# Gate and up of a SwiGLU FFN with seven block products in place of eight, in a two-layer hybrid network on one core

## The chip, the cores and the metric

The kernel runs on one core of a Trainium2 chip: TensorE (PE, with its weight loads as PEld), VectorE (DVE), ScalarE (ACT), GpSimd (POOL) and SyncE (SP), the last two here only to issue DMAs and for a few small fills. The metric is the device time of one launch in microseconds. Three runs of the kernel before gave 1988.75, 1989.3 and 1994.19 us.

## The reference

Two layers, 512 tokens, 1024 features, all in fp32. Each layer is

```
x = x + 0.5 * ffn(rms_norm(x), w_gate, w_up, w_down)      # "f1"
x = x + mixer(rms_norm(x))                                # "mx"
x = x + 0.5 * ffn(rms_norm(x), ...)                       # "f2"
ffn(x) = (silu(x @ w_gate) * (x @ w_up)) @ w_down         # 1024 -> 2816 -> 1024
rms_norm(x) = x * rsqrt(mean(x*x) + 1e-6) * w
```

The mixer concatenates an mLSTM, a state-space branch and a differential attention, and ends in a product with w_out. Its arithmetic is not changed.

## The kernel before

x stays in SBUF, transposed, as eight tiles x0 to x7 of 128 features by 512 tokens. Phases run in the order f1, mx, f2, f1, mx, f2.

Products are made in three parts: an fp32 operand is split into a high part that ScalarE casts to fp32r (L121 for weights, L134 for x) and the remainder that VectorE subtracts (L122, L135); `mm3` (L126 to L129) then issues three matmuls into one PSUM bank: high by high, high by low, low by high. The weights are the stationary operand, x the moving one, 512 tokens wide. In the mixer's token projections x is stationary and 256 or 272 columns of weights move.

The hidden layer has 22 blocks f of 128 features. For each f, gate and up take 2 x 8 products of a 128x128 weight block with a feature tile, 48 matmuls; then L212 to L220 make the hidden block: both sums are scaled by the inverse root `rsb`, silu, product, split into gh and gl. The down products, 8 x 22 x 3 = 528 matmuls, follow when all 22 blocks are there. An FFN is 1584 matmuls of 128x512.

When an output tile x[d] is complete, `prep` (L131 to L141) makes the next phase's xh[d] and xl[d] at once and adds x[d] squared to `sqacc`. The norm's factor is not applied to x but to the sums, so a phase's products can begin before it exists. For the first block of an FFN the order is written for this: gate and up run interleaved over the feature tiles, and the matmul that sums `sqacc` over the features (L176) stands before the eighth tile's products. VectorE's Newton steps for the inverse root (L151 to L156, eleven operations) then run beside TensorE.

Each engine executes its instructions in the order in which the framework's scheduler put them; instructions made under `tc.high_priority()` (weight loads, splits) are moved ahead. Weights come by 1 MB loads on SyncE's queue into two `raw` buffers; GpSimd's queue carries the DMAs that accumulate into SBUF. The mixer has four `big` buffers (NBIG) for its tables, sums and the decay tiles D of its four heads: `decay(h)` loads a mask into D, accumulates a row onto it by a GpSimd DMA (L759) and exponentiates it, `scores(h)` multiplies into it, `value(h)` (L784) uses it.

Of the kernel before, what the change touches and what calls it, by code (L numbers as in the profile page):

```python
# [30 lines left out]
NBIG = 4  # L31
# [13 lines left out]
def hybrid_kernel(ctx, tc, aps, phases):  # L45
# [4 lines left out]
    res = ctx.enter_context(tc.tile_pool(name="res", bufs=1))  # L50
    wp = ctx.enter_context(tc.tile_pool(name="wp", bufs=1))
# [29 lines left out]
    raw0 = None  # L81
    with tc.high_priority():

        nc.sync.dma_start(out=pv, in_=aps["pv"])
        if phases[0][0] != "mx":
            raw0 = wp.tile([P, 2048], F32, name="raw", tag="raw", bufs=2)
        for d in range(KD):
            if raw0 is not None and d in (0, 1, 3, 4):
                c = slice((0, 1024, 0, 512, 1536)[d], (512, 1536, 0, 1024, 2048)[d])
                nc.sync.dma_start(out=raw0[:, c], in_=aps["wgu"][phases[0][1], int(phases[0][0] == "f2"), 0][:, c])  # L90
            nc.sync.dma_start(out=x[d], in_=aps["xT"][:, d, :])
        nc.sync.dma_start(out=cn, in_=aps["cn"])
        nc.sync.dma_start(out=bc, in_=aps["bc"])
# [10 lines left out]
    def load(src, soon=True):  # L104
        n = src.shape[1]
        with tc.high_priority() if soon else nullcontext():
            raw = wp.tile([P, 2 * WPC], F32, name="raw", tag="raw", bufs=2)
            nc.sync.dma_start(out=raw[:, :n], in_=src)
        return raw

    def split(raw, lo, n, eng=dve):
        return split_parts(raw, ((lo, n),), eng)

    def split_parts(raw, parts, eng=dve):
        with tc.high_priority():
            hi = wp.tile([P, WPC], F32R, name="whi", tag="whi", bufs=3)
            lw = wp.tile([P, WPC], F32R, name="wlo", tag="wlo", bufs=3)
            to = 0
            for lo, n in parts:
                t = slice(to, to + n)  # L120
                act.copy(hi[:, t], raw[:, lo:lo + n])  # L121
                eng.tensor_tensor(lw[:, t], raw[:, lo:lo + n], hi[:, t].bitcast(F32), ALU.subtract)  # L122
                to += n
        return hi, lw

    def mm3(out, lh, ll, rh, rl, first, last):  # L126
        pe.matmul(out, lh, rh, start=first, stop=False)  # L127
        pe.matmul(out, lh, rl, start=False, stop=False)  # L128
        pe.matmul(out, ll, rh, start=False, stop=last)  # L129


    def prep(d, wcol):
        w = pv[:, wcol + d:wcol + d + 1]
        act.activation(xh[d], x[d], AF.Copy, scale=w)  # L134
        dve.scalar_tensor_tensor(xl[d], x[d], w, xh[d].bitcast(F32), ALU.mult, ALU.subtract)  # L135
# [7 lines left out]
    def rstd(ssq, n, pool_=tp, src=None):  # L143
# [5 lines left out]
        v = pool_.tile(shape, F32, name="rs_v", tag="rs_v%d" % w)  # L149
        q = pool_.tile(shape, F32, name="rs_q", tag="rs_q%d" % w)  # L150
# [22 lines left out]
    def rms_everywhere(pool_):  # L173

        ps = aux()
        pe.matmul(ps, ones, sqacc, start=True, stop=True)  # L176
        rstd(rsb, DM, pool_, ps)


    def ffn(l, which, nxt, first):  # L180
        with tc.tile_pool(name=f"g{l}{which}", bufs=1) as gp:
            gh, gl = [], []
            for f in range(KF):
                if f == 0:
# [24 lines left out]
                if first and 5 <= f <= 11 and f % 2:
                    spread_bias(f // 2 - 2)  # L210
# [767 lines left out]
```

## Time and profile before

| | |
|---|---|
| three runs | 1988.75, 1989.3, 1994.19 us |
| profiled execution: its own time, its span | 1989.71 us, 1987.6 us |
| busy: TensorE, VectorE, ScalarE, GpSimd | 1971.1, 1013.4, 696.7, 49.6 us |
| first matmul | 8.44 us |
| f1, mixer, f2 of layer 0 | 364.70, 263.50, 360.90 us |
| f1, mixer, f2 of layer 1 | 361.30, 264.00, 364.80 us |
| DMA: bytes moved, mean rate | 209.12 MB, 105 GB/s |
| granted TensorE clock over the span | 1.000 |

The span runs from the first to the last instruction of the profiled execution. The six stages are cut where the first matmul of a phase starts; the last one contains the output's stores. A matmul's listed duration overlaps that of its neighbours, so its cost in a stream is the distance from one start to the next.

### The profile page before, as it was taken

What the parts mean: (1) busy time and instruction counts of PE and PEld (TensorE: products, weight loads), DVE (VectorE), ACT (ScalarE), POOL (GpSimd) and SP (SyncE); (2) the same over time, 40 slices, a digit from 0 to 9 for tenths busy, and PEclk for the clock granted to TensorE, in tenths of its full rate; (3) what the DMA queues carried; (4) which work ended last, traced back from release to release, by engine and by line L of the source; (5) the groups of instructions that cost most, each with busy time, mean ns of one, the idle gap of its engine ahead of it and who ended that gap; (6) DMA issues with size and microseconds to landing.
All of it is one profiled execution on the core that took longest, in us unless ns stands there. A gap on an engine that the chain in (4) does not pass through costs nothing.

```text
span 1987.6 us, 23535 instructions
## 1 busy us (share of the span) xinstructions
PE 1971.1 (99%) x9598; PEld 1646.2 (83%) x9598; DVE 1013.4 (51%) x1697; ACT 696.7 (35%) x1140; POOL 49.6 (2%) x95
## 2 busy tenths in 40 slices
PE   8999999999999999999999999999999999999999
PEld 6888888989888888888888888889898888888887
DVE  7444433478765644443354444334877665444322
ACT  4223322347644322322223222223476333322211
POOL 0000000020000000000000000000200000000000
PEclk9999999999999999999999999999999999999999
DMA  5323232456412222223222222224654132232331
GB/s 181 119 99 104 87 106 85 134 165 159 112 49 88 103 90 101 103 88 106 85 106 85 106 86 106 91 91 139 189 136 101 42 106 103 89 107 85 111 102 63
DMA packets 48071, 209.12 MB, mean 105 GB/s; under 512 B 4871, under 2 KB 17447, under 8 KB 27100
## 3 DMA queue, kind: packets, MB, share of 16 engines
q1 hardware_dynamic: 41148, 187.38, 27.5%
q0 software_dynamic: 6816, 20.25, 4.3%
q8 instruction: 75, 1.23, 0.3%
q14 instruction: 32, 0.26, 0.0%
HBM read 194.97 MB, written 7.66 MB: 102 GB/s over the span
## 4 chain that ended last, share of the span: by engine, by line
PE 97%; DMA 1%; ACT 1%; DVE 0%; issue 0%; SPq 0%; POOLq 0%
PE acc L129 18%; PE acc L127 18%; PE acc L128 17%; PE aux L127 13%; PE aux L129 13%; PE aux L128 13%; PE po L566 1%; PE aux L784 1%; DMA D<-cn 1%; PE po L772 1%; PE aux L534 0%; DMA D<-row_dram 0%; PE aux L655 0%; PE aux L555 0%; PE side L772 0%; PE aux L707 0%
## 5 line engine op out<-in xcount | busy, mean ns | idle before, releaser
L121 ACT CAST whi<-raw 128x1024 fp32r<-128x1024 f32 (+2 forms) x344 | 350.8, 1022 | 984.5 <-PE acc L128 424.5
L122 DVE TENSOR_TENSOR wlo<-raw,whi 128x1024 fp32r<-128x1024 f32 (+2 forms) x344 | 407.4, 1187 | 329.3 <-ACT whi L121 329.1
L127 PE MATMUL acc<-xh,whi 128*128 128x512 f32 x896 | 353.1, 394 | 8.4 <-ACT xh L134 8.4
L128 PE MATMUL acc<-xl,whi 128*128 128x512 f32 x896 | 351.0, 392 | 0.0
L129 PE MATMUL acc<-xh,wlo 128*128 128x512 f32 x896 | 350.2, 391 | 0.0
L127 PE MATMUL aux<-xh,whi 128*128 128x512 f32 x704 | 274.2, 390 | 0.0
L129 PE MATMUL aux<-xh,wlo 128*128 128x512 f32 x704 | 274.2, 389 | 0.0
L128 PE MATMUL aux<-xl,whi 128*128 128x512 f32 x704 | 274.1, 389 | 0.0
L127 PEld LDWEIGHTS acc<-xh,whi 128*128 128x128 f32 x896 | 168.5, 188 | 43.6 <-ACT xh L134 8.4
L128 PEld LDWEIGHTS acc<-xl,whi 128*128 128x128 f32 x896 | 168.6, 188 | 34.9 <-issue 1.0
L129 PEld LDWEIGHTS acc<-xh,wlo 128*128 128x128 f32 x896 | 168.6, 188 | 34.2
L215 DVE TENSOR_TENSOR us<-aux,rsb 128x512 f32<-128x512 f32 x88 | 60.8, 691 | 265.0 <-PE aux L129 264.9
L128 PEld LDWEIGHTS aux<-xl,whi 128*128 128x128 f32 x704 | 132.3, 188 | 27.8
L129 PEld LDWEIGHTS aux<-xh,wlo 128*128 128x128 f32 x704 | 132.3, 188 | 27.6
L127 PEld LDWEIGHTS aux<-xh,whi 128*128 128x128 f32 x704 | 132.4, 188 | 27.3
L212 DVE TENSOR_TENSOR gs<-acc,rsb 128x512 f32<-128x512 f32 x88 | 60.8, 691 | 170.9 <-PE acc L129 170.8
L127 PE MATMUL acc<-gh,whi 128*128 128x512 f32 x352 | 138.7, 394 | 0.0
L127 PE MATMUL aux<-gh,whi 128*128 128x512 f32 x352 | 138.7, 394 | 0.0
L129 PE MATMUL acc<-gh,wlo 128*128 128x512 f32 x352 | 138.0, 392 | 0.0
L129 PE MATMUL aux<-gh,wlo 128*128 128x512 f32 x352 | 138.0, 392 | 0.0
L128 PE MATMUL acc<-gl,whi 128*128 128x512 f32 x352 | 136.6, 388 | 0.0
L128 PE MATMUL aux<-gl,whi 128*128 128x512 f32 x352 | 136.6, 388 | 0.0
(273 smaller groups left out, 2552.9 us busy)
## 6 DMA issues: line engine op xcount, KB each, us to landing
raw<-wgu SPq DMA_DIRECT2D x87, 1024.0 KB, 4.8
raw<-wdn SPq DMA_DIRECT2D x44, 1024.0 KB, 4.8
raw<-win SPq DMA_DIRECT2D x12, 1024.0 KB, 6.5
raw<-winf SPq DMA_DIRECT2D x12, 1024.0 KB, 4.9
raw<-wout SPq DMA_DIRECT2D x8, 1024.0 KB, 5.0
st<-qk_dram POOLq DMA_DIRECT2D x24, 256.0 KB, 5.8
sS<-cn SPq DMA_DIRECT2D x8, 512.0 KB, 4.8
qk_dram<-hl POOLq DMA_DIRECT2D x16, 256.0 KB, 3.3
```

The costliest lines, as they stand in the source:

```text
L121: act.copy(hi[:, t], raw[:, lo:lo + n])
L122: eng.tensor_tensor(lw[:, t], raw[:, lo:lo + n], hi[:, t].bitcast(F32), ALU.subtract)
L127: pe.matmul(out, lh, rh, start=first, stop=False)
L128: pe.matmul(out, lh, rl, start=False, stop=False)
L129: pe.matmul(out, ll, rh, start=False, stop=last)
L212: dve.tensor_tensor(gs, pp[0], rsb, ALU.mult)
L215: dve.tensor_tensor(us, pp[1], rsb, ALU.mult)
L566: pe.matmul(po[:, h * 64:(h + 1) * 64], at["a", n][:, j * P:(j + 1) * P], dv[j][:, (2 * p + h) * 64:(2 * p + h + 1) * 64], start=j == 0, s ...
L772: pe.matmul(sp[:, :n], mk[h // 2][hp, j * P:(j + 1) * P], mq[h // 2][hp, j * P:S], start=True, stop=True)
L784: pe.matmul(pnv[:, n, :], D[:, at_(j, n)], V[:, j, h, :], start=j == 0, stop=j == n)
```

## The change

Gate and up are computed by a Strassen-Winograd scheme. Two blocks of hidden features and the feature tiles in pairs make a 2x2 matrix of weight blocks (11, 12, 21, 22), the two halves of the tokens and the tile pairs a 2x2 matrix of x. Instead of eight block products there are seven, between blocks or sums of blocks. The 22 hidden blocks become 11 pairs p, and each pair is seven steps in the order of `STEPS`; a step is one weight block, or sum of blocks, of 128x1024 for gate and up together, split into high and low part, and 24 matmuls of 256 columns (2 for gate and up, 4 tile pairs, 3 parts). The sums of weights are s1 = 21 + 22 and s4 = 12 + s2, made by a GpSimd DMA that accumulates onto a loaded block, and s2 = 11 - s1, s3 = 11 - 21, made by VectorE. In the very first FFN, pairs 0 and 1 have s1 and s4 from VectorE. X, Y and Z name PSUM banks in which the products accumulate; copies of three partial results (`sn`) are added to others, one of them by an accumulating DMA (into c3).

The sums of x are made once for a phase: `prep7` scales two feature tiles, makes the three plain blocks xR (high and low) and the four sums xT (high and low). For the first FFN `prep_all` does all eight tiles at once.

The down products no longer wait for all hidden blocks. Six blocks at a time (18 matmuls into the bank `side`) are put between the steps of the next three pairs, by the table `WHEN`; the last four blocks' (12 matmuls for a feature tile) stand at the end. Loads are of 512 KB or less, into four `raw` and six `rx` buffers. The mixer keeps three `big` buffers in place of four; weights are laid out in memory to suit. The factor 0.5 moves from the addition to x into the hidden block.

```diff
-NBIG = 4
+NBIG = 3
+CB, RX, HB = 2, 6, 5
+WHEN = ((3, 4, 6, 7, 9, 10, 12, 13), (3, 5, 7, 9, 11, 13, 15, 17))
...
+    def prep7(i, wcol, tmp, four):
+        if i == 0:
+            parts["xR"] = [handed(4 + n, [P, 4, 2, 256], F32R, f"xR{n}") for n in range(3)]
+            parts["xT"] = []
+        xT = handed(i, [P, 4, 2, 256], F32R, "xT")
+        parts["xT"].append(xT)
+        xw = four("xw")
+        for n in range(2):
+            w = pv[:, wcol + 2 * i + n:wcol + 2 * i + n + 1]
+            act.activation(xw[:, 2 * n:2 * n + 2].rearrange("p a b -> p (a b)"), x[2 * i + n], AF.Copy, scale=w)
+        for n, b in enumerate((0, 2, 3)):
+            r = parts["xR"][n][:, i]
+            act.copy(r[:, 0], xw[:, b])
+            dve.tensor_tensor(r[:, 1], xw[:, b], r[:, 0].bitcast(F32), ALU.subtract)
+        sums(four("xt"), xw, xT, dve)
+        for n in range(2):
+            square(2 * i + n, tmp)
+    def sums(t, b, out, eng):
+        eng.tensor_tensor(t[:, 0], b[:, 1], b[:, 0], ALU.subtract)
+        eng.tensor_tensor(t[:, 1], t[:, 0], b[:, 3], ALU.subtract)
+        eng.tensor_tensor(t[:, 2], b[:, 3], b[:, 1], ALU.subtract)
+        eng.tensor_tensor(t[:, 3], b[:, 2], t[:, 1], ALU.add)
+        act.copy(out[:, :, 0], t)
+        dve.tensor_tensor(out[:, :, 1], t, out[:, :, 0].bitcast(F32), ALU.subtract)
...
-    def rms_everywhere(pool_):
-        ps = aux()
-        pe.matmul(ps, ones, sqacc, start=True, stop=True)
-        rstd(rsb, DM, pool_, ps)
-    def ffn(l, which, nxt, first):
...
+    STEPS = (("11", 0, "X"), ("s1", 3, "Y"), ("s2", 4, "X"), ("s4", 2, "Y"), ("s3", 5, "X"), ("12", 1, "Z"), ("22", 6, "X"))
+    def ffn(l, which, nxt, first, ctx3):
+        wcol = l * PV_N + (PV_N2 if which else PV_N1)
+        fp = ctx3.enter_context(tc.tile_pool(name=f"f{l}{which}", bufs=1, reuse_waits="tile"))
...
+        def blocks_of(p):
+            w = aps["wgu"][l, which, p]
+            soon = not first or p > 1
+            r = {"11": loadx(w[0], soon)}
+            if soon:
+                r["s1"] = loadx(w[2])
+                with tc.high_priority():
+                    pool.dma_start(out=r["s1"], in_=w[3], accum_op=ALU.add)
+            return r
+        def rest_of(p, r):
+            w = aps["wgu"][l, which, p]
+            soon = not first or p > 1
+            r["21"] = loadx(w[2], soon)
+            if soon:
+                r["s4"] = loadx(w[1])
+            r["12"] = load(w[1], soon)
+            r["22"] = load(w[3], soon)
+        def prep_all():
...
+            prep_all()
+        xR, xT = parts["xR"], parts["xT"]
+        hF = {}
+        def x_of(f, k):
+            return xR[f][:, k] if f < 3 else xT[k][:, f - 3]
+        def rms():
+            ps = side()
+            pe.matmul(ps, ones, sqacc, start=True, stop=True)
+            rstd(rsb, DM, (tmp(), tmp()), ps)
+        def gate_up(p, after):
+            raws = raws0 if first and p == 0 else blocks_of(p)
+            rest_of(p, raws)
+            c = cbig("c")
+            ps, copies = {}, {}
+            for n, (name, f, where) in enumerate(STEPS):
+                if name not in raws and name != "s2" and name != "s3":
+                    a, b = ("21", "22") if name == "s1" else ("12", "s2")
+                    raws[name] = fp.tile([P, WPC], F32, name=name, tag="rx", bufs=RX)
+                    dve.tensor_tensor(raws[name], raws[a], raws[b], ALU.add)
+                if name in ("s2", "s3"):
+                    a, b = (raws["11"], raws["s1"]) if name == "s2" else (raws["11"], raws["21"])
+                    with tc.high_priority():
+                        raws[name] = fp.tile([P, WPC], F32, name=name, tag="S", bufs=2)
+                        dve.tensor_tensor(raws[name], a, b, ALU.subtract)
+                        if name == "s2" and "s4" in raws:
+                            pool.dma_start(out=raws["s4"], in_=raws["s2"], accum_op=ALU.add)
+                hi, lw = split(raws[name], 0, 1024)
+                if name in ("11", "s1", "s2"):
+                    copies[name] = fp.tile([P, 2, 256], F32, name="sn", tag="sn", bufs=4)
+                for s in range(2):
+                    new = (s, where) not in ps
+                    if new:
+                        ps[s, where] = (total() if s and p % 2 else acc()) if where == "X" else aux()
+                    out = ps[s, where][:, 0:256]
+                    for k in range(4):
+                        cc = slice(s * 512 + k * P, s * 512 + (k + 1) * P)
+                        r = x_of(f, k)
+                        mm3(out, hi[:, cc], lw[:, cc], r[:, 0], r[:, 1], new and k == 0, k == 3, True)
+                    if name in copies:
+                        act.copy(copies[name][:, s], out)
+                    elif name == "s4":
+                        dve.tensor_tensor(c[:, s, 1], out, copies["s2"][:, s], ALU.add)
+                    elif name == "s3":
+                        act.copy(c[:, s, 3], out)
+                    elif name == "12":
+                        dve.tensor_tensor(c[:, s, 0], out, copies["11"][:, s], ALU.add)
+                    else:
+                        act.copy(c[:, s, 2], out)
+                if name == "s3":
+                    pool.dma_start(out=c[:, :, 3], in_=copies["s1"], accum_op=ALU.add)
+                after(n)
+            rb = rsb.rearrange("p (a b) -> p a b", b=256)[:, None].broadcast_to([P, 2, 2, 256])
+            g, u = c[:, 0], c[:, 1]
+            for t in (g, u):
+                t4 = t.rearrange("p (m n) t -> p m n t", m=2)
+                dve.tensor_tensor(t4, t4, rb, ALU.mult)
+            act.activation(g, g, AF.Silu)
+            dve.scalar_tensor_tensor(u, g, 0.5, u, ALU.mult, ALU.mult)
+            hh = fp.tile([P, 4, 256], F32R, name="hh", tag="hh", bufs=HB)
+            hl = fp.tile([P, 4, 256], F32R, name="hl", tag="hl", bufs=HB)
+            act.copy(hh, u)
+            dve.tensor_tensor(hl, u, hh.bitcast(F32), ALU.subtract)
+            hF[p] = [(hh[:, 2 * n:2 * n + 2].rearrange("p a b -> p (a b)"),
+                      hl[:, 2 * n:2 * n + 2].rearrange("p a b -> p (a b)")) for n in range(2)]
+        def down(c, d, ps):
+            fs = range(6 * c, min(6 * c + 6, KF))
+            n = len(fs) * P
+            raw = load(aps["wd3"][l, which, c, d] if c < 3 else aps["wd2"][l, which, d])
+            hi, lw = split(raw, 0, n)
+            for i, f in enumerate(fs):
+                cc = slice(i * P, (i + 1) * P)
+                mm3(ps, hi[:, cc], lw[:, cc], *hF[f // 2][f % 2], i == 0, i == len(fs) - 1)
+            dve.tensor_tensor(x[d], ps, x[d], ALU.add)
+            if c == 3:
+                if nxt is None:
+                    nc.sync.dma_start(out=aps["out"][:, d, :], in_=x[d])
+                elif nxt[0] == "mx":
+                    prep(d, nxt[1], tmp)
+                elif d % 2:
+                    prep7(d // 2, nxt[1], tmp, four)
+        todo = []
+        for p in range(KF // 2):
+            when = WHEN[p < 9]
+            base = 7 * (p % 3)
+            def after(n):
+                if p == 0 and n == 1:
+                    rms()
+                if first and p == 1 and n == 2:
+                    build_bias(lambda name: cbig(name).rearrange("p a b c -> p (a b c)"))
+                if first and p in (3, 4, 5, 6) and n == 1:
+                    spread_bias(p - 3)
+                for _ in range(when.count(base + n)):
+                    if todo:
+                        down(*todo.pop(0), side())
+            gate_up(p, after)
+            if p % 3 == 2:
+                todo += [(p // 3, d) for d in range(KD)]
+        while todo:
+            down(*todo.pop(0), side())
+        for d in range(KD):
+            down(3, d, aux() if d % 2 else acc())
...
```

On TensorE, at the entry into layer 0's f2, `yh`, `yl` belong to the mixer's last output tile, `sqacc` is the sum of squares, xh and xl (before) are the parts of a feature tile, xR (after) those of a plain block. Before, around the sum-of-squares matmul:

```order
2903 L127 MATMUL aux<-xh_95,whi 128x512
2904 L128 MATMUL aux<-xl_103,whi 128x512
2905 L129 MATMUL aux<-xh_95,wlo 128x512
2906 L176 MATMUL aux<-sqacc,ones 128x512
2907 L127 MATMUL acc<-xh_96,whi 128x512
2908 L128 MATMUL acc<-xl_104,whi 128x512
2909 L129 MATMUL acc<-xh_96,wlo 128x512
```

After, at the same matmul, now L306:

```order
3652 L115 MATMUL aux<-yh_6365,whi 128x512
3653 L116 MATMUL aux<-yl_6366,whi 128x512
3654 L117 MATMUL aux<-yh_6365,wlo 128x512
3655 L306 MATMUL side<-sqacc,ones 128x512
3656 L115 MATMUL acc<-xR_6383,whi 128x256
3657 L116 MATMUL acc<-xR_6383,whi 128x256
3658 L115 MATMUL acc<-xR_6383,whi 128x256
3659 L116 MATMUL acc<-xR_6383,whi 128x256
3660 L117 MATMUL acc<-xR_6383,wlo 128x256
```

Before, 42 matmuls of the first block lie between the mixer's last one (row 2863) and this one; after, it is the next instruction behind the mixer's last.

On VectorE at the same place, from the addition to the last feature tile on (L841 before); wlo is the low part of a weight block, sqacc the sum of squares, rs_v, rs_q and rsb the inverse root. Before:

```order
627 L841 TENSOR_TENSOR x_88<-aux,x_88 128x512
628 L122 TENSOR_TENSOR wlo<-raw,whi 128x1024
629 L135 SCALAR_TENSOR_TENSOR xl_104<-x_88,pv,xh_96 128x512
630 L141 TENSOR_TENSOR sqacc<-sqacc,sq 128x512
631 L122 TENSOR_TENSOR wlo<-raw,whi 128x1024
632 L151 TENSOR_SCALAR rs_v<-aux 128x512
633 L152 TENSOR_SCALAR rsb<-rs_v 128x512
634 L154 TENSOR_TENSOR rs_q<-rsb 128x512
635 L155 SCALAR_TENSOR_TENSOR rs_q<-rs_q,rs_v 128x512
636 L122 TENSOR_TENSOR wlo<-raw,whi 128x1024
```

After, six rows further behind the last addition (L126 is the sum of squares, L171 the low parts of the sums xT; sq takes the place of rs_v and rs_q, rx is the weight block "11"):

```order
759 L126 TENSOR_TENSOR sqacc<-sqacc,sq 128x512
760 L171 TENSOR_TENSOR xT<-xt,xT 128x4x256
761 L180 TENSOR_SCALAR sq<-side 128x512
762 L181 TENSOR_SCALAR rsb<-sq 128x512
763 L183 TENSOR_TENSOR sq<-rsb 128x512
764 L184 SCALAR_TENSOR_TENSOR sq<-sq 128x512
765 L185 SCALAR_TENSOR_TENSOR rsb<-sq,rsb 128x512
766 L111 TENSOR_TENSOR wlo<-rx,whi 128x1024
767 L183 TENSOR_TENSOR sq<-rsb 128x512
768 L184 SCALAR_TENSOR_TENSOR sq<-sq 128x512
769 L185 SCALAR_TENSOR_TENSOR rsb<-sq,rsb 128x512
770 L183 TENSOR_TENSOR sq<-rsb 128x512
```

Before, two low parts of weights stand ahead of the inverse root. After, the first low part of the phase stands behind five of its operations.

## Rows read from the trace of the kernel before

**Rows 1.** Page: busy time by engine, and the chain's shares by engine.
```profile
PE 1971.1 (99%) x9598; PEld 1646.2 (83%) x9598; DVE 1013.4 (51%) x1697; ACT 696.7 (35%) x1140; POOL 49.6 (2%) x95
...
PE 97%; DMA 1%; ACT 1%; DVE 0%; issue 0%; SPq 0%; POOLq 0%
```

**Rows 2.** Windows, one per FFN: length, then busy us of PE, PEld, DVE, ACT.
```profile
8.40:373.10 364.70, 364.66 (x1591) 299.37 (x1592) 168.55 (x206) 112.93 (x143) 2.82 (x5) 1.00 0.31 108
...
636.60:997.50 360.90, 360.90 (x1586) 297.52 (x1585) 160.13 (x190) 105.72 (x129) 0.00 (x0) 1.00 0.28 96
997.50:1358.80 361.30, 361.30 (x1588) 297.81 (x1588) 159.02 (x188) 103.62 (x127) 0.00 (x0) 1.00 0.27 95
...
1622.80:1987.60 364.80, 361.08 (x1586) 297.39 (x1584) 149.41 (x174) 95.00 (x111) 0.00 (x0) 1.00 0.26 93
```

**Rows 3.** Timeline of TensorE, 512 columns: start, duration; eleven in a row.
```profile
999.65 0.39 PE L127 MATMUL aux<-xh,whi 128*128 128x512 f32 x1
...
1001.92 0.39 PE L128 MATMUL acc<-xl,whi 128*128 128x512 f32 x1
```

**Rows 4.** Timeline of TensorE, 256 columns; twelve in a row.
```profile
394.39 0.28 PE L129 MATMUL acc<-whi,xl 128*128 128x256 f32 x1
...
395.71 0.28 PE L128 MATMUL acc<-wlo,xh 128*128 128x256 f32 x1
```

**Rows 5.** Timeline of TensorE from the first mixer into the second FFN.
```profile
636.15 0.39 PE L129 MATMUL aux<-yh,wlo 128*128 128x512 f32 x1
636.38 0.39 PE L127 MATMUL acc<-xh,whi 128*128 128x512 f32 x1
...
645.95 1.02 PE L176 MATMUL aux<-sqacc,ones 128*128 128x512 f32 x2
```

**Rows 6.** Timeline of VectorE in the same place.
```profile
636.58 0.69 DVE L841 TENSOR_TENSOR x<-aux,x 128x512 f32<-128x512 f32 x1 [2.42 <-PE aux L129]
...
647.06 0.69 DVE L151 TENSOR_SCALAR rs_v<-aux 128x512 f32<-128x512 f32 x1 [2.91 <-PE aux L176]
...
656.09 0.68 DVE L156 SCALAR_TENSOR_TENSOR rsb<-rs_q,rsb 128x512 f32<-128x512 f32 x1
```

**Rows 7.** Groups by line and shape: count, busy us, mean ns, idle before.
```profile
L122 DVE TENSOR_TENSOR wlo<-raw,whi 128x1024 fp32r<-128x1024 f32 x320 | 391.2, 1223 | 306.1 <-ACT whi L121 305.9
...
L121 ACT CAST whi<-raw 128x1024 fp32r<-128x1024 f32 x320 | 336.3, 1052 | 939.0 <-PE acc L128 417.9 <-issue 316.0 <-PE aux L128 171.8
...
L776 DVE TENSOR_TENSOR D<-side,D 128x256 f32<-128x256 f32 x8 | 3.3, 413 | 0.0
```

**Rows 8.** DMA issues: count, KB each, median us to landing.
```profile
raw<-wgu SPq DMA_DIRECT2D x87, 1024.0 KB, 4.8
...
sS<-row_dram POOLq DMA_DIRECT2D x8, 512.0 KB, 8.1
...
D<-cn SPq DMA_DIRECT2D x8, 256.0 KB, 2.8
D<-row_dram POOLq DMA_DIRECT2D x8, 256.0 KB, 5.1
```

**Rows 9.** Kernel start: window with clock; timeline of TensorE, seven in a row.
```profile
8.40:12.40 4.00, 3.96 (x9) 3.06 (x10) 3.62 (x7) 4.00 (x8) 0.00 (x0) 1.00 1.02 339
...
9.46 0.63 PE L128 MATMUL acc<-xl,whi 128*128 128x512 f32 x1
...
12.03 0.63 PE L129 MATMUL acc<-xh,wlo 128*128 128x512 f32 x1
```

**Rows 10.** Tile D in the first mixer: issue ns min/median/max, and its transfers.
```profile
L759 POOL DMA_DIRECT2D D<-row_dram x4: 872/872/872, 535.1 to 544.9; - x4
...
DMA to landing us min/median/max: 2.6/4.3/5.9
```

**Rows 11.** Chain of waits in the first mixer: start us, us, what.
```profile
571.26 4.41 PE aux L784 x40
```

More of the change, by code (lines that the diff above doesn't have):

```diff
@@ L72, in hybrid_kernel, with handed @@
     x = [res.tile([P, S], F32, name=f"x{d}") for d in range(KD)]
-    xh = [res.tile([P, S], F32R, name=f"xh{d}") for d in range(KD)]
-    xl = [res.tile([P, S], F32R, name=f"xl{d}") for d in range(KD)]
     sqacc = res.tile([P, S], F32, name="sqacc")
     rsb = res.tile([P, S], F32, name="rsb")
+    def handed(n, shape, dtype, name):
+        return hand.tile(shape, dtype, name=name, tag=f"a{n}")
+    parts = {}
     pv = const.tile([P, DEPTH * PV_N], F32, name="pv")
@@ L80, in hybrid_kernel @@
     bc = const.tile([P, DEPTH * BC_N], F32, name="bc")
[L81 to L93, printed above, removed]
     ident = cn[:, CN_ID:CN_ID + P]
@@ L117, in split_parts, with mm3, square @@
             lw = wp.tile([P, WPC], F32R, name="wlo", tag="wlo", bufs=3)
[L118 to L123, printed above, removed]
-        return hi, lw
[L126 to L135, printed above, removed]
+            act.copy(hi[:, :n], raw[:, lo:lo + n])
+            eng.tensor_tensor(lw[:, :n], raw[:, lo:lo + n], hi[:, :n].bitcast(F32), ALU.subtract)
+        return hi, lw
+    def mm3(out, lh, ll, rh, rl, first, last, skip=False):
+        pe.matmul(out, lh, rh, start=first, stop=False, skip_group_check=skip)
+        pe.matmul(out, lh, rl, start=False, stop=False, skip_group_check=skip)
+        pe.matmul(out, ll, rh, start=False, stop=last, skip_group_check=skip)
+    def square(d, tmp):
         if d == 0:
@@ L296, in t8, with tmp0, four @@
         def t8(name, tag):
+            at = {"y8": 4, "stq": 5, "stk": 6}.get(tag)
+            if at is not None:
+                return handed(at, [P, NB, S], F32, name)
             return mp.tile([P, NB, S], F32, name=name, tag=tag)
         def tmp(name, tag, bufs=2):
-            return (mp if tag == "tb" else tp).tile([P, S], F32, name=name, tag=tag, bufs=bufs)
+            return mp.tile([P, S], F32, name=name, tag=tag, bufs=bufs)
+        def tmp0():
+            return tmp("sq", "t0")
+        def four(name):
+            return mp.tile([P, 1280], F32, name=name, tag="big", bufs=NBIG)[:, 0:1024].rearrange("p (a b) -> p a b", b=256)
         def big(name):
@@ L859, in hybrid_kernel @@
     wcols = {"f1": PV_N1, "mx": PV_NM, "f2": PV_N2}
-    for d in range(KD):
-        prep(d, phases[0][1] * PV_N + wcols[phases[0][0]])
     for n, (kind, l) in enumerate(phases):
```

247 lines of the change are left out of this document (126 added, 121 removed).

## The prediction

> **What bounds the kernel now.** I read the page's busy shares and the chain by engine first [rows 1]: TensorE is busy 1971.1 of 1987.6 us, and 97% of the chain is its work, so the time is the number of matmuls times their spacing plus the places where TensorE waits. The stage table [rows 2] puts the places: each FFN takes 361 to 365 us, and TensorE is idle in almost none of it, while VectorE works 150 to 169 us and ScalarE 95 to 113 us of the same stretch. A view in order of time then gives the spacing, which is what counts, since a matmul's own 0.39 us overlaps its neighbours: ten steps from 999.65 to 1001.92 are 0.227 us for 512 columns [rows 3], and eleven from 394.39 to 395.71 are 0.120 us for 256, each with its own weight load, in the mixer's token projection [rows 4]. An FFN of 1584 matmuls is 1584 x 0.227 = 359.6 us, so what is not matmul is 1.3 us in the third stage, 1.7 in the fourth, 5.1 in the first; the last has some 3.9 us of output tail besides [rows 2].
>
> Why that is so little is seen where a mixer ends. The last output matmul starts at 636.15 and the first FFN matmul at 636.38 [rows 5]: that one needs only the first feature tiles, which are long ready. The sum of squares is waited for by a matmul at 645.95, and VectorE's inverse root after it, 647.06 to 656.8, is a reason for nobody to wait [rows 5, 6].
>
> **What goes: matmul time.** Gate and up lose 22 x 48 = 1056 matmuls of 512 columns (1056 x 0.227 = 239.7 us) and get 11 pairs x 7 steps x 24 = 1848 of 256 columns (1848 x 0.120 = 221.8 us). The down products stay 528 of 512. That is -17.9 us for an FFN, -72 us for four. The bound from below is the same spacing with no wait anywhere; I take the row because it has the shape, the weight load and the data type. The Trainium skill (TensorE: Matmul & The Clock Gate, "Back-to-back issue gap") gives an isolated gap of N/2.4 + 2.5 ns. By that, estimated, 512 columns would be 216 ns and 256 columns 109 ns, and the saving would be 1056 x 0.216 - 1848 x 0.109 = 26.7 us for an FFN, 107 in all. This trace has 227 and 120 ns, 11 more on each, and since there are more and shorter matmuls afterwards those 11 ns count against the change.
>
> **What comes in the steady state.** A pair needs from VectorE 7 lo parts, 2 differences of weights (s2, s3), two scalings, a product and a lo part of the hidden block, all of 1024 columns (13 x 1.22), and four adds of 0.41 on 256 columns: 17.5 us [rows 7]. TensorE works 168 x 0.120 = 20.2 us on a pair alone and about 31 us where downs stand between. ScalarE has nine operations of 1024 columns by 1.05 [rows 7] and ten copies of 256, some 13 us. So VectorE has 2.7 us to spare in the pairs without downs and more in the others. The sums s1 and s4 and the late add c3 go by accumulating DMAs: 512 KB took 8.1 us and 256 KB 5.1 us to land [rows 8], and s4's is needed some 20 us after its issue, the others nearly as long. The loads rise from 1 MB to about 3 MB for 256 hidden features in 20 to 31 us, and 1 MB landed in 4.8 us [rows 8]. I take 0.1 us lost for a pair, 4 us for 44, and 0.5 us at each of four ends, where copy, two scalings and both parts of the last hidden block (about 5.3 us) lie beside one 18-matmul down and six matmuls (5.4 us): +6. The bounds are 0 and 0.5 us for a pair, 22.
>
> **What is moved: the entry of each FFN.** Here the cover goes. All seven steps of pair 0 need xR or xT of all eight feature tiles, where the old first block began with the first. And in the instruction order the whole sum-of-squares matmul now stands directly behind the last matmul of the stage before, and VectorE's queue has that stage's last sums, then five operations of the inverse root, and only then the lo part of block "11". Count from E, the end of the last output matmul. Add to x 0.7, scaling on ScalarE 0.7, three sums, two lo parts and the square's add (5 x 0.41 + 0.7), with the hand-overs: squares summed at E + 4.4. The matmul and its release take 1.1 (645.95 to 647.06), so the root starts near E + 5.7. Its eleven operations and two lo parts took 9.7 us before, some 0.67 an operation, so five end at E + 9.1 and the lo part of "11" at E + 10.3 [rows 5, 6]. TensorE has only four matmuls to do until then. After such a wait I let the first 4 us run at the lower of its two clock levels: at the start of this kernel, after TensorE had done nothing, the matmuls from 9.46 to 12.03 stand 0.428 us apart, the 1.2 GHz spacing, though the granted-clock column of that stretch reads 1.00 [rows 9]. That ends step "11" at E + 15.4. Behind its lo part stand four more root operations (2.7), two differences (2.4) and s1's lo part (1.2): s1 runs from E + 16.6, s2 until E + 22.4. The difference s2 is ready at E + 14.2, and only then can the DMA that makes s4 go: 0.9 + 8.1 us [rows 8, 10], then cast 1.05 and lo part 1.22, E + 25.5. From there 4 steps of 2.9 us: pair 0 ends at E + 37.1 instead of 20.2, an excess of 16.9 us for 1.3 before: **+15.6, twice**. If that DMA takes the 2.6 us of the mixer's fastest 256 KB [rows 10] and the clock stays up it is +8; if it takes 13 beside the loads, +22.
>
> The Trainium skill (GPSIMD Engine Reference, Specifications) says that GpSimd's SBUF interfaces are shared with VectorE and contended when VectorE has two SBUF inputs, which is every lo part here. The trace does not bear it out for issuing a DMA: in the mixer 4 issues took 0.872 us each at shortest, median and longest [rows 10]. By the rule an issue could wait one such operation, 1.2 us more in each of three entries.
>
> From the second FFN into the third, VectorE is late before the entry already: during the last eight downs (8 x 12 x 0.227 = 21.8 us) it has 9 adds, 6 half lo parts, a full one, 28 of 256 columns, 7 adds of squares and 4 of 1024 columns: 5.7 + 3.8 + 1.2 + 10.9 + 4.4 + 4.8 = 30.8 us. The sums end at E + 10, the lo part of "11" at E + 16.7, s4 can start at E + 31.7, and pair 0 ends at E + 42.8: excess 22.6 for 1.7, **+20.9** (13 to 27).
>
> The first FFN: VectorE makes all xR and xT from 7.5 us on, about 36 operations of 256 to 512 columns and three of 1024, 25 us, before s1's lo part. TensorE can do "11" and then waits from about 21 to 35; pair 0 ends near 54 instead of 8.4 + 20.2. With 3 us for a small bias matmul in pair 1, which waits for a bank that VectorE frees, that is 28.4 for 5.1, **+23.3** (15 to 30).
>
> **What is taken away.** With three large buffers instead of four, the fourth decay tile's load waits for value(0), whose matmuls start the 40 of 571.26 [rows 11]; before, it had a buffer of its own. Load 2.8, issue 0.9, accumulate 5.1 [rows 8], one exponential and a product are 9.8 us, beside 7.6 us of value and score work: +2.2 for a mixer, **+4.4** (0 to 12).
>
> **Sum.** -72 + 31.2 + 20.9 + 23.3 + 4.4 + 6 = +14. On the profiled execution's 1989.7 us (span 1987.6 and 2.1 around it; the median of the runs is 0.4 lower) that is 2004 us. With every bound at its low end it is -72 + 16 + 13 + 15 = -28, 1962; at its high end -72 + 44 + 27 + 30 + 12 + 24 = +65, 2055.
>
> **Rivals.** *Short entries.* The mechanism is the same queue, with half the price: if the accumulating DMA lands in 3 to 4 us and VectorE fills its waits, an entry costs 9 to 14 us; the point from which it decides is 56 us more for the four entries, where the sum above has 75. For it: VectorE's independent operations stand only 0.61 us apart. Against it: the row order fixes who comes first. All four shortened by 8 us give 1972, faster. *Covered.* The entries are hidden as before and only the matmuls count: 1989.7 - 72 + 12 = 1930. Against it stands the order of both engines. *Even.* Entries about 14 us lower in sum: 1989. *Starved pairs.* VectorE at 87% in order with ScalarE, and three accumulating DMAs for a pair, cost 1 us a pair: 2004 + 40 = 2044. For it: each step's cast stands in ScalarE's queue among result copies that wait for TensorE; against it the 20 us of slack. *Not what it says:* if 256 columns were bound by the 188 ns of a weight load, gate and up would take 347 us; the token projection excludes it.
>
> **Chances.** Forecast 0.42 (its own range 1996 to 2018), short entries 0.22, even 0.16, starved 0.14, covered 0.06. The range of 1966 to 2034 leaves out most of covered and starved. Within 0.3% (6 us, about what a measurement can tell from none) is the even case: 0.16; faster 0.28; slower 0.56.
>
> **What would show it.** In the profile after: a spacing of 0.120 us in gate and up; TensorE idle for about 10 us after a mixer, 16 after the second FFN and 14 in the first, around the sum-of-squares matmul, and again before s4, released by a lo part; FFN stages near 372, 360, 366 and 364 us are the forecast, near 380, 370, 376 and 374 starved pairs; pairs 1 to 10 without gaps over 0.5 us. I am wrong if pair 0 takes less than 28 us after a mixer, or if pairs in the middle wait.

## The result: 83 us slower

The changed kernel takes 2072.9 us (2072.01 to 2073.94) where the kernel before takes 1989.54: a ratio of 1.0414, with a 95% interval of 1.0396 to 1.0432. The forecast was 2004 in a range of 1966 to 2034. The direction was right; the size was not, and the sum had next to nothing for its main cause.

The page of the profiled execution, against [rows 1]: busy time by engine, the granted clock in forty slices, and the DMA issues of the FFNs with their size and median time to landing.

```profile
span 2071.1 us, 32422 instructions
...
PE 1965.3 (95%) x12766; PEld 1779.7 (86%) x12766; DVE 1418.3 (68%) x2157; ACT 986.0 (48%) x1732; POOL 176.7 (9%) x223
...
PEclk8899999999999899999989999999999989999999
...
rx<-wgu POOLq DMA_DIRECT2D x42, 512.0 KB, 7.6
rx<-s POOLq DMA_DIRECT2D x42, 512.0 KB, 6.1
...
c<-sn POOLq DMA_DIRECT2D x44, 256.0 KB, 6.2
```

TensorE is busy 6 us less for 72 us less of matmuls at full rate: part of its time now runs at the lower clock level. The stages, cut where the last matmul of the phase before ends (in the kernel before that is where the next phase's first one starts), against [rows 2] (length, then busy us of PE, PEld, DVE, ACT and POOL, then the granted clock):

```profile
6.80:390.60 383.80, 360.38 (x2382) 330.84 (x2383) 273.34 (x334) 187.97 (x301) 33.44 (x38) 0.96 0.59 160
390.60:660.30 269.70, 266.64 (x1626) 229.32 (x1624) 193.87 (x484) 141.59 (x323) 21.75 (x39) 0.98 0.43 119
660.30:1039.30 379.00, 359.13 (x2379) 331.98 (x2378) 254.52 (x295) 174.96 (x270) 32.70 (x33) 0.96 0.61 164
1039.30:1418.30 379.00, 354.30 (x2380) 327.32 (x2380) 257.31 (x292) 174.15 (x267) 32.97 (x35) 0.97 0.59 156
1418.30:1687.90 269.60, 266.58 (x1626) 229.45 (x1624) 193.92 (x484) 141.42 (x323) 22.96 (x41) 0.98 0.43 122
1687.90:2071.10 383.20, 358.24 (x2379) 330.74 (x2378) 244.50 (x270) 163.09 (x247) 32.73 (x33) 0.96 0.59 158
```

Each FFN lost 18 to 19 us (forecast: -1 to +7) and each mixer 6.

Where in an FFN? Each pair of hidden blocks is taken from its first matmul to the next pair's (pair 0 from the stage's start), less its matmuls at full rate (256 columns by 0.120 us, 512 by 0.227). What is left, its excess in us, in the order f1, f2, f1, f2:

| | f1 | f2 | f1 | f2 | sum |
|---|---|---|---|---|---|
| pair 0, forecast | 25.4 | 16.9 | 22.6 | 16.9 | 81.8 |
| pair 0, measured | 24.0 | 19.6 | 23.9 | 17.4 | 84.9 |
| pairs 1 to 3, measured | 14.7 | 14.4 | 10.1 | 16.4 | 55.6 |
| pairs 4 to 10, measured | 3.0 | 2.9 | 2.9 | 3.1 | 11.9 |

For all pairs but the first the forecast had 9 us, bias product included. Pairs 1 to 3 alone have 55.6. Of the 69 us between forecast and result, some 51 lie in pairs 1 to 3, 7 in pairs 4 to 10, 7 in the mixers and 3 in the entries.

One such place is the step from pair 2 into pair 3 in layer 0's f2. GpSimd's queue, VectorE, ScalarE and TensorE in order of time (start us, duration, what; in brackets the idle time before and its releaser), a fence for each:

```profile
742.41 0.88 POOL L234 DMA_DIRECT2D rx<-wgu  x1 [6.32 <-DVE c L341]
743.50 1.21 POOL L349 DMA_DIRECT2D c<-sn  x1 [0.20 <-issue]
```

```profile
745.72 1.22 DVE L111 TENSOR_TENSOR wlo<-rx,whi 128x1024 fp32r<-128x1024 f32 x1 [0.35 <-ACT whi L110]
755.68 1.23 DVE L355 TENSOR_TENSOR c<-c,rsb 128x1024 f32<-128x1024 f32 x1 [8.73 <-DMA c<-sn]
756.83 1.22 DVE L111 TENSOR_TENSOR wlo<-s,whi 128x1024 fp32r<-128x1024 f32 x1
```

```profile
748.48 0.37 ACT L347 COPY c<-acc 128x256 f32<-128x256 f32 x1
756.94 1.06 ACT L356 ACTIVATE c<-c 128x1024 f32<-128x1024 f32 x1 [8.10 <-DVE c L355]
757.90 0.35 ACT L339 COPY sn<-acc 128x256 f32<-128x256 f32 x1
```

```profile
753.08 0.28 PE L117 MATMUL aux<-xT,wlo 128*128 128x256 f32 x1
758.31 0.58 PE L115 MATMUL acc<-xT,whi 128*128 128x256 f32 x1 [4.95 <-ACT sn L339]
758.91 0.41 PE L117 MATMUL acc<-xT,wlo 128*128 128x256 f32 x1
759.12 0.41 PE L115 MATMUL acc<-xT,whi 128*128 128x256 f32 x1
```

The DMA that adds s1's copy into c3 is issued 1.1 us behind the 512 KB one for the next pair's s1, and the scaling L355 that needs c3 begins only 12.2 us later. c3's transfer consists of 256 packets of 1 KB, and its first ones come some 5 us behind its issue: of packets between 512 B and 2 KB the DMA view counts none from 744 to 748 us, 247 from 748 to 753 and 9 from there to 755.6. Ahead of them GpSimd's queue moves the 512 KB in front. VectorE stands before the scaling, with the next pair's low parts behind it in its queue. ScalarE stands before the silu, with the copy of the next pair's step "11" (L339) behind it. TensorE may not add s2 into that bank until the copy is made. So a wait for one DMA passes through two queues into the next pair's third step. Over the kernel, the group of these scalings (count, busy us, mean ns, idle before and its releasers) has the line below; 72.5 of its 95.9 us stand at the scalings of pairs 0 to 2.

```profile
L355 DVE TENSOR_TENSOR c<-c,rsb 128x1024 f32<-128x1024 f32 x88 | 107.5, 1221 | 99.9 <-DMA c<-sn 95.9 <-ACT c L347 4.0
```

And the wait is paid twice. Windows before, in and behind it (columns as above; the last three numbers are the granted clock, the DMA engines' busy share, and GB/s):

```profile
747.40:753.00 5.60, 5.60 (x49) 5.60 (x48) 0.00 (x0) 1.32 (x2) 0.00 (x0) 1.00 1.06 305
753.00:758.30 5.30, 0.36 (x4) 0.16 (x2) 2.62 (x3) 1.36 (x3) 0.00 (x0) 0.87 0.10 37
758.30:763.00 4.70, 4.69 (x22) 4.69 (x23) 4.70 (x5) 2.78 (x6) 0.90 (x1) 0.50 0.23 34
```

Until 753 all DMA engines are busy (305 GB/s, loads for the most part), and c3's transfer has its share of them; what is left of it then lands with 0.10 of them busy. TensorE idles, and runs its next 4.7 us at 0.50, the 1.2 GHz level: 22 matmuls at 0.21 us. Over the four FFNs the 256-column matmuls that stand 0.15 to 0.30 us apart add up to 31 us above 0.120, entries included.

### The profile page after: what moved, and what is told of

It is laid out like the page before. It is cut to its first block, busy times and chain, and to the rows that moved or that the text cites. A ratio compares the mean times of both kernels' runs of the same rounds, so it can differ in the third digit from the quotient of the medians.

```text
span 2071.1 us, 32422 instructions
## 1 busy us (share of the span) xinstructions
PE 1965.3 (95%) x12766; PEld 1779.7 (86%) x12766; DVE 1418.3 (68%) x2157; ACT 986.0 (48%) x1732; POOL 176.7 (9%) x223
## 3 DMA queue, kind: packets, MB, share of 16 engines
q0 software_dynamic: 30880, 75.83, 20.2%
## 5 line engine op out<-in xcount | busy, mean ns | idle before, releaser
L110 ACT CAST whi<-raw 128x768 fp32r<-128x768 f32 (+3 forms) x288 | 265.0, 920 | 383.4 <-PE side L116 215.3
L111 DVE TENSOR_TENSOR wlo<-raw,whi 128x768 fp32r<-128x768 f32 (+3 forms) x288 | 305.2, 1060 | 108.3 <-ACT whi L110 107.1
L115 PE MATMUL acc<-xT,whi 128*128 128x256 f32 x816 | 237.2, 291 | 29.8 <-ACT sn L339 26.2
L117 PE MATMUL acc<-xT,wlo 128*128 128x256 f32 x816 | 234.6, 288 | 5.0 <-DVE wlo L111 5.0
L116 PE MATMUL acc<-xT,whi 128*128 128x256 f32 x816 | 235.0, 288 | 0.0
L115 PE MATMUL side<-hh,whi 128*128 128x512 f32 x576 | 229.2, 398 | 0.0
L117 PE MATMUL side<-hh,wlo 128*128 128x512 f32 x576 | 226.9, 394 | 0.0
L116 PE MATMUL side<-hl,whi 128*128 128x512 f32 x576 | 225.8, 392 | 0.0
L115 PE MATMUL aux<-xR,whi 128*128 128x256 f32 x704 | 200.5, 285 | 2.0 <-ACT sn L339 1.9
L116 PE MATMUL aux<-xR,whi 128*128 128x256 f32 x704 | 200.0, 284 | 0.0
L115 PEld LDWEIGHTS acc<-xT,whi 128*128 128x128 f32 x816 | 160.8, 197 | 35.2 <-ACT sn L339 28.0
L355 DVE TENSOR_TENSOR c<-c,rsb 128x1024 f32<-128x1024 f32 x88 | 107.5, 1221 | 99.9 <-DMA c<-sn 95.9
L116 PEld LDWEIGHTS acc<-xT,whi 128*128 128x128 f32 x816 | 161.0, 197 | 2.0
L115 PEld LDWEIGHTS aux<-xR,whi 128*128 128x128 f32 x704 | 136.1, 193 | 3.6 <-ACT sn L339 2.6
L116 PEld LDWEIGHTS aux<-xR,whi 128*128 128x128 f32 x704 | 136.0, 193 | 1.1
```

The source lines that it names most:

```text
L110: act.copy(hi[:, :n], raw[:, lo:lo + n])
L111: eng.tensor_tensor(lw[:, :n], raw[:, lo:lo + n], hi[:, :n].bitcast(F32), ALU.subtract)
L115: pe.matmul(out, lh, rh, start=first, stop=False, skip_group_check=skip)
L116: pe.matmul(out, lh, rl, start=False, stop=False, skip_group_check=skip)
L117: pe.matmul(out, ll, rh, start=False, stop=last, skip_group_check=skip)
L355: dve.tensor_tensor(t4, t4, rb, ALU.mult)
```

## Experiments

Excess of pair 0 and of pairs 1 to 3 over their matmuls, for the four FFNs (us, worked out as above), and the mixers' lengths:

| kernel | time | pair 0 | pairs 1 to 3 | mixers |
|---|---|---|---|---|
| changed kernel | 2072.9 | 24.0, 19.6, 23.9, 17.4 | 14.7, 14.4, 10.1, 16.4 | 269.7, 269.6 |
| c3_dve | 2030.7 | 24.0, 17.5, 23.2, 17.4 | 14.6, 0.2, 0.2, 0.2 | 266.6, 272.5 |
| sums_dve | 2020.7 | 23.3, 12.5, 16.0, 12.4 | 9.1, 2.4, 5.1, 7.1 | 271.1, 268.2 |
| s4_p0_dve | 2071.2 | 24.5, 15.2, 16.7, 14.8 | 16.4, 15.7, 16.7, 17.7 | 269.6, 269.4 |
| nbig4 | 2058.7 | 24.7, 17.8, 23.6, 17.1 | 13.6, 13.5, 11.6, 15.9 | 263.5, 263.7 |
| p0_dve | 2014.9 | 24.8, 12.5, 16.0, 12.2 | 13.7, 5.4, 0.8, 7.1 | 265.2, 264.0 |
| no_acc | 1997.5 | 25.0, 12.5, 15.3, 12.6 | 8.5, 1.9, 0.2, 1.9 | 263.3, 263.7 |
| p0_rms | 2001.1 | 23.9, 6.8, 10.3, 6.9 | 5.5, 8.1, 8.4, 8.5 | 263.4, 265.5 |
| p0_rms_bias | 2002.5 | 24.5, 6.8, 10.4, 6.9 | 12.1, 8.0, 7.7, 5.7 | 263.5, 263.8 |
| na_small | 1982.2 | 26.2, 10.2, 13.7, 8.8 | 1.9, 0.3, 0.3, 0.3 | 263.6, 266.0 |
| na_hp_small | 1985.5 | 27.4, 10.6, 14.3, 10.6 | 2.0, 0.5, 0.4, 0.5 | 263.7, 263.2 |
| p0_small | 1988.1 | 27.0, 9.5, 13.1, 9.9 | 4.9, 0.6, 0.2, 1.7 | 263.6, 266.4 |

c3_dve, p0_rms_bias and na_small have several runs and an interval, and these runs lie up to 4.5 us apart; the others are single runs, read by their stages.

**c3_dve: the last sum by VectorE.**

```diff
-                        act.copy(c[:, s, 3], out)
+                        dve.tensor_tensor(c[:, s, 3], out, copies["s1"][:, s], ALU.add)
...
-                if name == "s3":
-                    pool.dma_start(out=c[:, :, 3], in_=copies["s1"], accum_op=ALU.add)
```

> The changed kernel, but the last sum of a pair (c3 = s3's result + the copy of s1's) is made by VectorE out of PSUM, two adds of 256 columns, in place of a ScalarE copy and an accumulating DMA. Theory A: VectorE, which works in order, stands before the first scaling of a pair until that DMA has landed, and holds the low parts of the next pair behind it; then the idle time before the scaling goes and pairs 1 to 3 of each FFN lose their 10 to 16 us: 2018 to 2035 us. Rival B: pairs without downs are short of VectorE time; then two more adds (0.8 us a pair) make it 2073 to 2085. Rival C: what pairs 1 to 3 lose is the backlog of the entry; then 2065 to 2073.

2030.68 us (ratio to before 1.0201, 1.0184 to 1.0218). Pairs 1 to 3 of three FFNs go from 10 to 16 us to 0.2. The scalings, now L353, wait 4.6 us in all, and for no DMA:

```profile
L353 DVE TENSOR_TENSOR c<-c,rsb 128x1024 f32<-128x1024 f32 x88 | 107.3, 1219 | 4.6 <-ACT c L347 4.6
```

VectorE has more to do and TensorE waits less, so theory A holds for 42 of the 83 us, 40 of them in pairs 1 to 3, and B and C fall. In the first FFN the 14.6 us stay, although VectorE had waited 14 us for c3 there: in c3_dve it waits 7.3 us in pair 2 for a DMA that makes an s1 (13.7 us from issue to landing), and pair 1 keeps its 7.3 us with s1 and s4 from VectorE.

**sums_dve: the sums of weights by VectorE, c3's DMA kept.** It drops the loads and DMAs of `blocks_of` and `rest_of` that make s1 and s4, so that the path of the first two pairs serves all.

> The changed kernel, but the sums of weights s1 and s4 of all pairs by VectorE (as the first two pairs of the first FFN have it), no accumulating DMA onto weights; c3's stays. Theory A: the wait for c3 stays and VectorE has 2.4 us more a pair: 2075 to 2110. Rival D: c3's DMA lands late (6.2 us) since the sums' DMAs of 512 KB go ahead of it in the same queue; then it lands in 3 to 5 us and the kernel is faster, 2030 to 2060.

2020.7, better than both expectations: D goes the right way. c3's DMA lands in 5.3 us instead of 6.2 at the median and VectorE waits 41.5 us for it instead of 95.9:

```profile
L348 DVE TENSOR_TENSOR c<-c,rsb 128x1024 f32<-128x1024 f32 x88 | 107.4, 1220 | 46.6 <-DMA c<-sn 41.5 <-ACT c L340 4.2 <-ACT sn L332 0.9
```

Pairs 1 to 3 lose 32 us less. That the queue alone is the cause is not shown, since the edit also takes away loads that share the DMA engines, and c3's DMA still takes up to 10.2 us with no sum in front of it. Another 20 us of the gain are in pair 0, 5 to 8 us in each of the last three FFNs, where s1 and s4 no longer wait for DMAs. That VectorE has 2.4 us more work a pair does not show.

**s4_p0_dve: only pair 0's s4 by VectorE** (`if soon and p > 0:` for its load).

> The changed kernel, but in pair 0 of every FFN s4 = 12 + s2 by VectorE in place of the accumulating DMA. If the entry's end is set by that DMA as the prediction's sum had it, pair 0 of the last three FFNs is 4 to 8 us shorter each: 2050 to 2061. If it is set by what stands before it on VectorE (inverse root, first low parts), less than 2 us each: 2067 to 2075.

The time is that of the second case, but its reason is not. Pair 0 did get 2.6 to 7.2 us shorter in the last three FFNs, 14 in all, so s4's DMA did set its end; and 11 us came back in pairs 1 to 3. VectorE's wait for c3 rises from 95.9 to 105.2 us, which is most of these 11: the wait for c3 swallowed what the entry gained.

**nbig4: four large buffers in the mixer** (`NBIG = 4`).

> The changed kernel with four large buffers in the mixer in place of three. The mixers went from 263.5 and 264.0 us to 269.7 and 269.6. If the lost buffer is the cause, they come back to about 264 and the time is 2061 us; if it is the prediction's share alone (the fourth decay tile), 2068; if neither, 2073.

2058.7: both mixers are back at 263.5 and 263.7. The lost buffer cost 12 us, not 4.4. The traces show which tile pays: in the changed kernel's first mixer TensorE has one long wait, for sS, the last of four tiles of sums that also lie in the large buffers, and 2 us later it runs 10.3 us at 0.50:

```profile
563.70 0.41 PE L823 MATMUL aux<-XC,sS 128*128 128x64 f32 x2 [1.97 <-DVE sS L818]
```

```profile
565.80:576.10 10.30, 10.30 (x30) 7.20 (x29) 4.78 (x9) 4.97 (x17) 0.86 (x1) 0.50 0.42 78
```

The second mixer has the same (1.84 us at 1591.32, 10.3 us at 0.50). In nbig4 VectorE's last product into sS begins at 553.4 instead of 564.1, TensorE does not wait there, and both mixers have a granted clock of 1.00. For the decay tile of the forecast TensorE waits nowhere longer than 0.3 us.

**p0_dve: c3 by VectorE, four buffers, pair 0's s1 and s4 by VectorE.**

> c3 by VectorE (as in c3_dve, 2031 us), four large buffers in the mixer, and pair 0 of every FFN makes s1 and s4 by VectorE, with block 22 loaded ahead of block 12. If what pair 0 saved in s4_p0_dve (14 us over three FFNs) was only given back to the wait for c3, it stays saved now that this wait is gone: 2031 - 9 (mixers) - 14 to 20 = 2002 to 2008. If pairs 1 to 3 hold it back in another way: 2015 to 2022.

2014.9, at the lower edge of the second case. Pair 0 keeps its 5 to 7 us, but pair 1 gets 5.2 and 6.9 us after the mixers, where c3_dve has none (in the first FFN it has 7.9, for 7.3 there).

**no_acc: as p0_dve, but s1 and s4 of all pairs by VectorE.**

> c3 by VectorE, four large buffers, and s1 and s4 of all pairs by VectorE: no accumulating DMA in the FFNs. VectorE then has 17.5 + 2.4 + 0.8 = 20.7 us of work in a pair without downs, where TensorE has 20.2. If VectorE's time bounds these pairs, pairs 1 and 2 lose 0.5 to 3 us each against p0_dve and it is 2006 to 2025; if not, the two are within 3 us.

1997.5, 17 us below p0_dve: the opposite of what a VectorE bound would give. The ideal 20.2 us of pairs without downs are reached with 20.7 us of counted VectorE work beside them, since its independent operations follow each other closer than their listed durations (1.13 to 1.14 us from start to start, as at 647.00 to 649.27 below).

**p0_rms: the inverse root held back to behind s1.**

```diff
+            held = (tmp(), tmp())
+            for t in held:
+                act.copy(t[:, 0:1], out[:, 0:1])
...
-            rstd(rsb, DM, (tmp(), tmp()), ps)
+            rstd(rsb, DM, held, ps)
```

> As p0_dve, but the Newton steps of the inverse root cannot begin before s1's product: their two work tiles are held until then by a copy of one column of it. If the entry waits for the low part of block 11 because that stands behind five of these steps, pair 0 is 3 to 4 us shorter after a mixer and after the second FFN: 9 to 13 us less than p0_dve. If the late steps only move the wait to the end of the pair (scaling), no gain.

2001.1, 14 us below p0_dve. Pair 0 is 5.3 to 5.7 us shorter in the last three, more than expected, and pairs 1 to 3 take back 2.7, 7.6 and 1.4: the place in VectorE's order sets the entry, and most of it stays gained after a mixer only. This is 5 of the 14 us. The other 9 are in the first FFN (24.8 + 13.7 to 23.9 + 5.5), and the next run, with the same edit, does not repeat them; their cause is open.

**p0_rms_bias: the bias product's tiles from other buffers.**

> As p0_rms, but the small bias product of pair 1 of the first FFN takes its two work tiles from the squares' buffers in place of the two hidden-sum buffers c, of which the pairs need both. If these cost pairs 1 and 2 of the first FFN their 7.3 and 7.1 us, it is 8 to 14 us less than p0_rms and at or below the kernel before (1980 to 1992); if not, within 3 us of p0_rms.

2002.52 (ratio 1.0056, 1.0040 to 1.0073): within 2 us of p0_rms. The first FFN's pairs 1 and 2 have 11.9 us, where p0_rms has 5.2 and not the 14.4 of c3_dve that the expectation counted with. These tiles are not the cause.

**na_small: no accumulating DMA, and the small inverse root.**

```diff
-            ps = side()
-            pe.matmul(ps, ones, sqacc, start=True, stop=True)
-            rstd(rsb, DM, (tmp(), tmp()), ps)
+            spread(rms_of_x())
```

> As no_acc (no accumulating DMA in the FFNs, four large buffers; 1997.5 us), and the inverse root is made as the mixer makes it: sums of squares to a 128x4 tile, eleven operations on 4 columns, spread back by TensorE and one ScalarE copy, in place of eleven operations on 512 columns (7.4 us of VectorE). If VectorE's queue sets the length of the entries, pair 0 of the last three FFNs (12.5, 15.3, 12.6 us over) is 5 to 7 us shorter each, with nothing given back in pair 1 (as it was in p0_rms): 1977 to 1984, below the kernel before. If the entry is set by the sum of squares' wait or by loads: 1994 to 1998.

1982.15 us over five rounds: ratio 0.996 (0.9946 to 0.9973), 0.4% below the kernel before and 91 us below the changed one. The entry into layer 0's f2, TensorE and then VectorE:

```profile
642.80 0.40 PE L117 MATMUL aux<-yh,wlo 128*128 128x512 f32 x1
647.89 0.39 PE L115 MATMUL acc<-xR,whi 128*128 128x256 f32 x1 [4.69 <-ACT whi L110]
649.41 0.58 PE L117 MATMUL acc<-xR,wlo 128*128 128x256 f32 x1 [0.51 <-DVE wlo L111]
```

```profile
647.00 1.22 DVE L171 TENSOR_TENSOR xT<-xt,xT 128x1024 fp32r<-128x1024 f32 x1
648.14 1.22 DVE L111 TENSOR_TENSOR wlo<-rx,whi 128x1024 fp32r<-128x1024 f32 x1
649.27 1.22 DVE L309 TENSOR_TENSOR s<-rx,raw 128x1024 f32<-128x1024 f32 x1
...
657.03 0.16 DVE L180 TENSOR_SCALAR rs_v<-rst 128x4 f32<-128x4 f32 x1
```

The low part of "11" stands right behind x's last sums, and an operation of the root takes 0.16 us. Pair 0 gains 2.3, 1.6 and 3.8 us against no_acc, half of what was expected, pairs 1 to 3 another 1.6, 0 and 1.6, and the first FFN 5.4 in all: the time lies in the expected range in part by gains that were not in its sum.

**na_hp_small: the sums of weights moved ahead.**

> As na_small, with VectorE's sums s1 and s4 at high priority, which in the first FFN puts them ahead of the sums of x that later steps need. If the first FFN's 25 us in pair 0 are s1's place behind all of these sums, it is 4 to 6 us less than na_small; if the sums only exchange places on a full engine, within 2 us or more by the sums of pair 1 that then go ahead too.

1985.5: the first FFN is not better (27.4 in pair 0), the others 0.4 to 1.8 worse. The sums only exchange places. In na_small VectorE works on x from 7.5 to 30.2 us, with s1's sum between, and s1's low part begins behind that at 32.4; that this order alone sets the 26 us is argued, not tested.

**p0_small: accumulating DMAs from pair 1 on, small inverse root.**

> As p0_dve (accumulating DMAs for s1 and s4 from pair 1 on; 2014.9 us) with the small inverse root. Pair 0 gets shorter as in na_small, and pair 1's 5 to 8 us stay if they are the wait for the DMA that makes its s1: 1994 to 2002. If they were the inverse root's backlog, it ends beside na_small, under 1985.

1988.1, under the expected range and above na_small. Pair 1's excess after a mixer falls from 5.2 and 6.9 to 0.4 and 1.5 us, and in no_acc, with the long root but without the DMAs, it is 1.6 and 1.6. So in p0_dve it took both, the DMA that makes s1 and the inverse root's backlog in VectorE's queue. Only the first FFN keeps 4.7 us there.

## Why the prediction was wrong

The mechanism that the forecast named was there, at its place and nearly at its size; another one, which it had priced at almost nothing, brought most of the 69 us that were missing.

*Matmul time: right.* 256-column steps stand 0.120 us apart at the higher clock level in the changed kernel, as in [rows 4]. Downs are 0.233 apart, where the old downs were 0.229; this makes most of the 3 us a FFN in pairs 4 to 10.

*Entries: right in kind and order, in one of them by luck.* With E = 660.3, the forecast had the squares summed at E + 4.4, the root from E + 5.7, the low part of "11" at E + 10.3, s1's at E + 16.6 and s4's at E + 25.5. VectorE, against [rows 6]:

```profile
663.67 0.69 DVE L126 TENSOR_TENSOR sqacc<-sqacc,sq 128x512 f32<-128x512 f32 x1
...
666.17 0.69 DVE L180 TENSOR_SCALAR sq<-side 128x512 f32<-128x512 f32 x1 [0.68 <-PE side L306]
...
669.42 1.22 DVE L111 TENSOR_TENSOR wlo<-rx,whi 128x1024 fp32r<-128x1024 f32 x1
...
675.03 2.36 DVE L323 TENSOR_TENSOR s<-rx 128x1024 f32<-128x1024 f32 x2 [1.62 <-DMA rx<-wgu]
677.31 1.22 DVE L111 TENSOR_TENSOR wlo<-rx,whi 128x1024 fp32r<-128x1024 f32 x1
...
686.35 1.23 DVE L111 TENSOR_TENSOR wlo<-rx,whi 128x1024 fp32r<-128x1024 f32 x1 [5.36 <-ACT whi L110]
```

Their ends are E + 4.1, (start) 5.9, 10.3, 18.2 and 27.3: right until s1's DMA, which was late by 1.6. (s4's DMA took 8.2 us from the start of its issue to the cast; the forecast's 0.9 + 8.1 has the issue twice, since the time to landing already runs from its start.) TensorE, against [rows 5], waits where it was said:

```profile
664.41 1.73 PE L306 MATMUL side<-sqacc,ones 128*128 128x512 f32 x2 [3.94 <-DVE sqacc L126]
...
670.69 0.58 PE L117 MATMUL acc<-xR,wlo 128*128 128x256 f32 x1 [3.70 <-DVE wlo L111]
```

The four pairs 0 cost 84.9 us over their matmuls, forecast 81.8. In layer 1's f1, behind the second FFN (E = 1039.3), the near hit is luck. VectorE was sooner there than forecast, with the low part of "11" at E + 14.3 instead of 16.7 and s4's at E + 26.6 instead of 31.7; then VectorE stood 5.1 us before the next pair's difference s2, which is moved ahead in its queue and needs that pair's s1, whose DMA took 12.4 us from issue to landing (1058.44 to 1070.88). The low part of pair 0's s3 stood behind it, and the pair ended at E + 44.5 instead of 42.8. The sum had no such wait:

```profile
1070.95 1.23 DVE L323 TENSOR_TENSOR s<-rx 128x1024 f32<-128x1024 f32 x1 [5.08 <-DMA rx<-wgu]
...
1073.37 0.58 PE L117 MATMUL acc<-xT,wlo 128*128 128x256 f32 x1 [4.30 <-DVE wlo L111]
```

*Steady state: the step that failed.* It said of the accumulating DMAs: "s4's is needed some 20 us after its issue, the others nearly as long", took 0.1 us for a pair, and named 0.5 us as the upper bound. For s4 and s1 that is so behind the first pair: no wait of VectorE or ScalarE for their DMAs shows there. It is false for c3: its DMA can only be issued when s3's product is copied, two steps of 2.9 us before the pair's end, and the scaling waits for it right there. The 0.5 us of the upper bound has no working behind it that follows this chain. The rows on hand show that there was no slack: 5.1 us from issue to landing for 256 KB [rows 8], against two steps, 5.8 us, less a copy of 0.4 us, and pairs 0 to 2 of each FFN have no downs to hide what comes on top. Measured it was 6.2 us at the median, up to 12.1 behind other transfers, and 42 us of the kernel went with it in c3_dve. The starved pairs had been a rival at 2044 with a chance of 0.14. It named the in-order queues and the three accumulating DMAs, but not the one that comes late, and priced them at 40 us; its other part, VectorE's own time, no_acc excludes.

*Clock.* The drop to the lower level was counted once for an entry, 4 us long. Behind the mixer of layer 0 the granted clock was 0.53 from 664.4 to 670.7, 0.50 from there to 674.9, and 0.86 in the rest of the pair. Matmuls behind the waits of pairs 0 to 2 ran at it too, as at 758.31.

*Mixers: undersized, and by another tile.* 11.8 us for 4.4, through sS and the clock behind its wait and not through the fourth decay tile, as nbig4 shows. The forecast had no term for the clock there.

On what the Trainium skill states: the Trainium skill (TensorE: Matmul & The Clock Gate, "Back-to-back issue gap") would have, by estimate, 109 ns at 256 columns; the changed kernel has 120. Issues on GpSimd as a rule did not wait for an operation of VectorE (1.2 us, as weighed in the prediction): the 42 of s4's DMAs took 0.86 to 0.93 us each, and of the 42 of s1's four took 1.07 to 1.23. For the DMA that decided, the Trainium skill (DMA: Bandwidth & Descriptors, "Anatomy of one DMA — SWDGE (gpsimd) path") fits 2.0 us plus bytes over 436e3, 2.6 us for 256 KB; the trace has 6.2. By the page's figure, an estimate, c3 would have been on time.

What stays open: the wider spacing of the downs, and the first FFN's pairs 1 and 2, which gave way in full (from 14 to 2 us) only when neither DMAs nor the long inverse root were left.

## What to carry to other kernels

When work is put on a DMA because the arithmetic engine is full, write down for each such DMA when its input exists, when its output is needed, and which engine's queue stands before that need: a late result in front of an in-order engine holds everything behind it, also for the next block. An engine at 87% by summed durations can be the cheaper place, as c3_dve and no_acc show here. And a gain at one place of such a chain (s4_p0_dve) may not show until the next wait is gone.

## What the runs showed that was not expected

- The accumulating DMAs took 6.2 us (256 KB, 4.7 to 12.1) and 6.1 to 7.6 us (512 KB) at the median between SBUF tiles or from memory; moving them all to VectorE took 75 us from the kernel (2072.9 to 1997.5, four mixer buffers included).
- An 11-operation Newton chain costs VectorE 7.4 us on 128x512 and some 2.2 us on 128x4 (0.20 from start to start).
